# A hybrid decoder block: early column pairs of the MLP dealt out among the others, buffers and DMA order of the second MLP product rearranged

## The chip, the cores and the metric

One core of one Trainium2 chip runs the whole kernel. The metric is device time in microseconds (us) of one execution; the figure given for a kernel is the median of its timed runs. Engines are named as the profile names them: PE is the matmul engine, DVE the vector engine, ACT the scalar engine, POOL is GpSimd, and SP issues DMAs. L1120 is line 1120 of the kernel before.

## The reference, cut to what matters

```
h = RMSNorm(x); three attention branches of h, merged by gates      # first half of the kernel
x = x + merged @ w_out                                              # 1024 x 1024
h = RMSNorm(x)                                                      # gain g_mlp
hid = square(relu(h @ w_mlp_in))                                    # 1024 x 4096, "up"
x = x + hid @ w_mlp_out                                             # 4096 x 1024, "down"
return RMSNorm(x)                                                   # gain g_final
```

There are 1024 tokens of width 1024, all fp32. The change touches only what follows the branches: the output projection, the MLP and the last norm.

## The kernel before

**Products.** Every fp32 operand is split into a high part, which ACT copies with rounding (L97: `hi_…`, `th`, `sh`), and a low part, which DVE or POOL makes by a subtraction (L982: `lo_…`, `tl`, `sl`). A product is then three matmuls per step of the contraction, hi·hi, lo·hi and hi·lo (lines L152 to L154).

**The MLP by Strassen.** Both MLP products are cut in 2 x 2 blocks and made with seven block products instead of eight. In the up phase the 4096 columns of `hid` are 16 *pairs* c (128 columns from each of two neighbouring groups), and each pair needs seven products of 12 matmuls of 128x512 (`times`, output `mb_u` or `tb_u` in PSUM). The tiles `T2`, `T3`, `T4` and the halves of `h2T` are the token side. The weight side is made by `load_pair`: DMAs bring raw blocks r0 to r3, POOL adds them in four instructions (L1089 to L1092), ACT and DVE split the sums (`s23`, `s1`, `s4`, and `a1` for the unsummed block). All of r1 and r2 rotate in two buffers named `xn`, which the normalised token tiles used before; r3 and `ud` (the split s4) have one buffer each.

**Early pairs.** Two of the seven products of a pair need only token half 1. For the pairs c < EARLY they run ahead (`mb_ep`, `mb_eq`, 24 matmuls a pair) while token half 2 is being normalised, transposed (`tb_h`) and combined into T2 to T4. Their results are parked in DRAM (`p1_d`, `hid_d[0]`). In the up phase such a pair has five products (60 matmuls), any other seven (84). The up phase takes the pairs in the order 0 to 15.

**The end of a pair.** DVE adds the products, ACT does relu and square, POOL makes four differences `ta`, `tb` (L1152 to L1158), and seven blocks go to DRAM as `hid_d[k]`, k = 0 to 6, all issued by SP (L1120).

**Down phase.** The groups of blocks are [0], [5, 3], [4, 2], [6], [1]. Each block has four sub-steps sc of 48 matmuls. For a sub-step, SP loads a 1 MB raw tile `tr` from `hid_d[k][sc]` (L1218) and raw weight tiles `wr` of 0.5 MB (L1178); for the groups of two blocks POOL adds weight tiles (L1182, 40 instructions); ACT makes `sh` and `th`, DVE `sl` and `tl`, and PE multiplies (`mb_dn`, `tb_dn`). Raw `tr` tiles rotate in two buffers (`braw`), which lie in a pool that exists already in the up phase; 14 of the `wr` buffers lie in pool E, which takes the space that the up phase's pool M (T2 to T4, `stg`, `ud`) leaves.

**Last norm.** `finish` computes r = 1/rms with small DVE instructions (a Newton iteration); then one half of a token tile is scaled on DVE in one instruction, the other on ACT (x·r, L977) and POOL (·gain, L978), and both go out.

**Output projection.** It runs in four quarters (token half, column half); `load_x` brings the residual x for a quarter, 4 DMAs, at the third of four steps of the quarter.

**Order.** The code is written in program order, and a scheduler puts each engine's instructions (and SP's DMAs) into one fixed order by its own estimate of times; `band("w")` and `band("crit")` set priorities in it. On the chip every engine works its list strictly in order, so a DMA on SP waits for all those ahead of it on SP to have been issued.

Of the kernel before, what the change touches and what calls it, by code (L numbers as in the profile page):

```python
# [22 lines left out]
P = 128  # L23
# [10 lines left out]
NEG_BIG = -float(2.0 ** 117)  # L34
POS_BIG = float(2.0 ** 117)
DSA_AHEAD = 2
EARLY = 10
MERGE_WITH = (range(4), range(4, 6), range(6, 8), ())
GATE_ORDER = [*range(8), *range(16, 24), *range(8, 16)]
GATES_EARLY = 10  # L40
# [14 lines left out]
def kernel(  # L55
# [929 lines left out]
    for tg in range(2):  # L985
        ss = X3.tile([P, 2, 16], F32, tag="n_ss4", name=f"ss2_{tg}", bufs=2)[:, :, :4]
        for n in range(2):
            cs = slice(n * 512, (n + 1) * 512)
            banks = [mb_bank(f"o{tg}{n}{i}") for i in range(4)] if tg or n else first_banks
            for kp in range(KT // 2 if tg or n else 0):  # L990
                if kp == 2:
                    load_x(tg, n)
                out_part(tg, n, banks, kp)
            with band("crit"):
                for i in range(4):
                    t = 4 * tg + i
                    nc.vector.tensor_tensor(x2[:, t, cs], banks[i], x2[:, t, cs], op=ALU.add)
                    jk = X3.tile([P, 512], BF16, tag="junk", name=f"jk2_{t}{n}")
                    nc.scalar.activation(jk, x2[:, t, cs], AF.Square, accum_out=ss[:, n, i:i + 1])
        if tg:  # L1000
            ctxG.close()
            M = ctxM.enter_context(tc.tile_pool(name="M", bufs=1, side="right", reuse_waits="tile"))
            T2, T3, T4 = ([M.tile([P, 4, 512], F32R, tag=f"{nm}_{part_}", name=f"{nm}_{part_}") for part_ in ("hi", "lo")]
                          for nm in ("T2", "T3", "T4"))
        with band("crit"):
            nc.vector.tensor_tensor(ss[:, 0], ss[:, 0], ss[:, 1], op=ALU.add)
            r = rsqrt_newton(X3, ss[:, 0], 4, f"h2_{tg}")
            for i in range(4):
                t = 4 * tg + i
                ts = slice(i * P, (i + 1) * P)  # L1010
                xn = X3.tile([P, D], F32, tag="xn", name=f"xn{t}", bufs=2)
                tps = []
                for half in range(2):
                    hs = slice(half * 512, (half + 1) * 512)
                    scale_half(half, xn[:, hs], x2[:, t, hs], r[:, i:i + 1], g2[:, hs])
                    tp = tb_bank(f"h2{t}{half}")
                    for k in range(4):
                        nc.tensor.transpose(tp[:, k * P:(k + 1) * P],
                                            xn[:, (4 * half + k) * P:(4 * half + k + 1) * P], ident)
                    tpv = tp.rearrange("p (k c) -> p k c", k=4)  # L1020
# [29 lines left out]

    for c in range(EARLY):
        a11, a12 = halves(load_unit(wcol[2 * c], f"wi{2 * c}", nc.vector))
        ps1, ps2 = mb_bank(f"ep{c}"), mb_bank(f"eq{c}")
        st = M.tile([P, 2, 512], F32, tag="stg", name=f"st{c}", bufs=2)
        product(ps1, a11, B11)
        act_copy(st[:, 0], ps1)
        product(ps2, a12, B21)
        nc.vector.tensor_tensor(st[:, 1], ps2, st[:, 0], op=ALU.add)
        nc.scalar.activation(st[:, 1], st[:, 1], AF.Relu)
        nc.scalar.activation(st[:, 1], st[:, 1], AF.Square)  # L1060
        with band("w"):
            nc.sync.dma_start(p1_d[c], st[:, 0])
            nc.sync.dma_start(hid_d[0][c // 4][:, c % 4], st[:, 1])

    ring = {"n": 0}

# [32 lines left out]
    def up_pair(c):  # L1099
# [15 lines left out]
            nc.scalar.activation(v, v, AF.Relu, scale=scale)  # L1115
            nc.scalar.activation(v, v, AF.Square)

        def out_block(k, v):
            with band("w"):
                nc.sync.dma_start(hid_d[k][c // 4][:, c % 4], v)  # L1120


        last = c == NPAIR - 1
        m6 = times(s2, T2)
        if last:
            m7, m4 = times(s3, T3), times(a22, T4)
# [7 lines left out]
        if c >= EARLY:  # L1134
            vadd(c11, times(a12, B21), c11)
            square(c11)
            out_block(0, c11)
        else:
            with band("w"):
                nc.sync.dma_start(c11, hid_d[0][c // 4][:, c % 4])  # L1140
        vadd(c21, m4 if last else times(a22, T4), c22)
        m5 = times(s1, T1)
        vadd(c22, m5, c22)
        vadd(c12, m5, c12)
        square(h[:, 2:4])
        vadd(c12, times(s4, N22), c12)
        square(c12, -1.0)
        sub = partial(nc.gpsimd.tensor_tensor, op=ALU.subtract)
        ta, tb = (M.tile([P, 2, 512], F32, tag="stg", name=f"t{nm}{c}", bufs=2) for nm in ("a", "b"))
        out_block(1, c21)  # L1150
        out_block(2, c22)
        sub(ta[:, 0], c12, c11)  # L1152
        out_block(3, ta[:, 0])
        sub(ta[:, 1], c22, ta[:, 0])
# [3 lines left out]
        sub(tb[:, 1], c21, ta[:, 1])  # L1158
        out_block(6, tb[:, 1])

    for c in range(NPAIR):
        up_pair(c)

    ctxM.close()
# [6 lines left out]
    n_raw, n_op, n_bank = [0], [0], [0]  # L1171

    def w_block(i, j, c0):
        n = n_raw[0]
        n_raw[0] += 1
        pool, tag, bufs = (X3, "xn", 2) if n < 2 else ((base, "st_raw", 1), (X3, "w3_raw", 1))[n - 2] if n < 4 else (E, "wr", 14)
        raw = pool.tile([P, 2, 512], F32, tag=tag, name=f"wr{n}", bufs=bufs)
        nc.sync.dma_start(raw, w2[:, c0:c0 + 2, j - 1, (i - 1) * 512:i * 512])  # L1178
        return raw

    def add(o, a, b):
# [23 lines left out]
    def down_group(blocks, weights, evict):
# [115 lines left out]
```

## Time and profile before

| | us |
|---|---|
| timed, median of 3 runs (lowest, highest) | 1480.31 (1479.31, 1480.57) |
| the profiled execution's own time | 1476.49 |
| its span, first to last instruction | 1474.4 |
| PE busy | 1397.2 (95%) |
| DVE busy | 1041.8 (71%) |
| POOL busy | 659.4 (45%) |

The profile shows one execution, and its span is 2.1 us shorter than its own time. PE is the busiest engine by far, so the time can be read as PE's work plus the gaps in it; a gap on another engine matters only if it makes one on PE. Everything up to about 743 us runs from the same instruction lists in both kernels.

### The profile page before, as it was taken

How to read it: one execution, taken by the hardware profiler on the slowest of the kernel's cores; microseconds unless marked ns; L12 is line 12 of the kernel's file. 1: busy time of each engine (PE TensorE's matmuls, PEld its weight loads, DVE VectorE, ACT ScalarE, POOL GpSimd, SP SyncE). 2: the span in 40 equal slices, each digit the busy share in tenths (PEclk: the TensorE clock that was granted, in tenths of full speed). 3: DMA queues.
4: the chain of work that ended last, by engine and by line, in shares of the span. 5: the costliest groups of instructions: out<-in, count | busy, mean ns of one | idle time of the engine just before them, and what ended most of it. 6: DMA issues, size and time to landing. Idle time of an engine off the chain costs nothing. (4 is left out here: it accounts for less than half of the span.)

```text
span 1474.4 us, 19857 instructions
## 1 busy us (share of the span) xinstructions
PE 1397.2 (95%) x6806; PEld 1174.0 (80%) x6806; DVE 1041.8 (71%) x1871; ACT 753.4 (51%) x1397; POOL 659.4 (45%) x526
## 2 busy tenths in 40 slices
PE   6999999998899999999999999989998799999997
PEld 5788877897788898788778888777887577778885
DVE  7667999999997665756744775455444599975954
ACT  5545777875456554463535664344444333433542
POOL 4231223425667533353525236767653579730101
PEclk9999999999999999999999999999999899999999
DMA  6212331312211114346463466666445978875421
GB/s 222 86 58 83 96 103 44 97 40 62 57 44 55 58 45 145 116 147 190 159 227 102 147 191 209 203 207 207 163 151 179 363 275 276 287 256 206 170 94 57
DMA packets 169815, 216.56 MB, mean 147 GB/s; under 512 B 14036, under 2 KB 102132, under 8 KB 166132
## 3 DMA queue, kind: packets, MB, share of 16 engines
q1 hardware_dynamic: 169716, 215.31, 44.6%
q8 instruction: 53, 0.87, 0.3%
q14 instruction: 46, 0.38, 0.1%
HBM read 162.32 MB, written 52.95 MB: 146 GB/s over the span
## 5 line engine op out<-in xcount | busy, mean ns | idle before, releaser
L152 PE MATMUL gt_g<-hT_hi,hi_g 128*128 128x512 f32 x384 | 151.7, 395 | 2.8 <-DVE gs L831 2.2
L153 PE MATMUL gt_g<-hT_lo,hi_g 128*128 128x512 f32 x384 | 151.9, 396 | 0.2 <-DVE hT_lo L219 0.2
L154 PE MATMUL gt_g<-hT_hi,lo_g 128*128 128x512 f32 x384 | 151.4, 394 | 0.0
L982 DVE TENSOR_TENSOR tl<-tr,th 128x1024 fp32r<-128x1024 f32 x56 | 107.7, 1930 | 57.0 <-ACT th L97 55.1
L152 PE MATMUL mb_dn<-sh,th 128*128 128x512 f32 x336 | 132.6, 396 | 12.6 <-ACT th L97 12.6
L1182 POOL TENSOR_TENSOR wr<-wr,wr 128x1024 f32<-128x1024 f32 x40 | 123.5, 3094 | 43.7 <-DMA wr<-in_w_mlp_out_dram 42.4
L153 PE MATMUL mb_dn<-sl,th 128*128 128x512 f32 x336 | 132.9, 397 | 2.2 <-DVE sl L982 2.2
L154 PE MATMUL mb_dn<-sh,tl 128*128 128x512 f32 x336 | 130.7, 393 | 1.7 <-DVE tl L982 1.7
L97 ACT ACTIVATE th<-tr 128x1024 fp32r<-128x1024 f32 x56 | 58.5, 1051 | 137.7 <-PE tb_dn L153 114.2
L982 DVE TENSOR_TENSOR sl<-wr,sh 128x1024 fp32r<-128x1024 f32 x56 | 96.8, 1733 | 12.4 <-ACT sh L97 12.3
L544 DVE TENSOR_SCALAR_CACHE_REDUCE tk_jk<-isc,tk_c 128x384 bf16<-128x384 f32 (+3 forms) x128 | 103.5, 809 | 2.5
L111 POOL TENSOR_TENSOR lo_g<-raw_g,hi_g 128x1024 fp32r<-128x1024 f32 x24 | 58.2, 2424 | 94.6 <-ACT hi_g L97 85.7
L541 ACT ACTIVATE tk_jk<-isc,tk_c 128x1024 bf16<-128x1024 f32 x64 | 73.6, 1149 | 29.4 <-DVE tk_c L553 26.6
L97 ACT ACTIVATE hi_s<-r 128x1024 fp32r<-128x1024 f32 (+1 forms) x48 | 43.2, 911 | 85.0 <-POOL r L1090 35.6
L152 PEld LDWEIGHTS gt_g<-hT_hi,hi_g 128*128 128x128 f32 x384 | 72.4, 189 | 17.4 <-DVE gs L831 2.7
L152 PEld LDWEIGHTS mb_dn<-sh,th 128*128 128x128 f32 x336 | 64.2, 191 | 27.4 <-ACT th L97 13.9
L153 PEld LDWEIGHTS gt_g<-hT_lo,hi_g 128*128 128x128 f32 x384 | 72.4, 189 | 13.9 <-DVE hT_lo L219 0.5
L154 PEld LDWEIGHTS gt_g<-hT_hi,lo_g 128*128 128x128 f32 x384 | 72.4, 189 | 13.4
L152 PE MATMUL mb_u<-T_hi,hi_s 128*128 128x512 f32 x192 | 75.3, 392 | 7.4 <-ACT hi_s L97 7.4
L153 PEld LDWEIGHTS mb_dn<-sl,th 128*128 128x128 f32 x336 | 64.2, 191 | 17.7 <-DVE sl L982 4.6
L978 POOL TENSOR_TENSOR x<-x,g_final_t 128x512 f32<-128x512 f32 x8 | 11.4, 1431 | 148.7 <-ACT x L977 148.7
L154 PEld LDWEIGHTS mb_dn<-sh,tl 128*128 128x128 f32 x336 | 63.8, 190 | 15.9 <-DVE tl L982 2.6
(469 smaller groups left out, 4262.1 us busy)
## 6 DMA issues: line engine op xcount, KB each, us to landing
wr<-in_w_mlp_out_dram SPq DMA_DIRECT2D x80, 512.0 KB, 5.5
tr<-hid_d SPq DMA_DIRECT2D x28, 1024.0 KB, 7.1
raw_g<-in_w_in_dram SPq DMA_DIRECT2D x24, 512.0 KB, 4.0
g_d<-gs SPq DMA_DIRECT2D x48, 256.0 KB, 2.0
gl<-g_d SPq DMA_DIRECT2D x48, 256.0 KB, 3.4
hid_d<-hid SPq DMA_DIRECT2D x38, 256.0 KB, 3.5
raw_wo<-in_w_out_dram SPq DMA_DIRECT2D x16, 512.0 KB, 3.5
r<-in_w_mlp_in_dram SPq DMA_DIRECT2D x32, 256.0 KB, 3.9
```

The source lines that it names most:

```text
L97: nc.scalar.activation(o, i, AF.Copy)
L111: lo_engine.tensor_tensor(lo, raw, hi.bitcast(F32), op=ALU.subtract)
L152: nc.tensor.matmul(ps, st_hi, mv_hi, start=first, stop=False)
L153: nc.tensor.matmul(ps, st_hi, mv_lo, start=False, stop=False)
L154: nc.tensor.matmul(ps, st_lo, mv_hi, start=False, stop=last)
L541: nc.scalar.activation(jk[:, :n], isc[t], AF.Sign, bias=cand_f[:, j:j + 1], scale=-1.0, accum_out=cnt[:, j:j + 1])
L544: nc.vector.tensor_scalar(jk[:, :n], isc[t], cand_f[:, j:j + 1], 0.0, op0=ALU.is_ge, op1=ALU.add, accum_out=cnt[:, j:j + 1])
L978: nc.gpsimd.tensor_tensor(o, o, g, op=ALU.mult)
L982: engine.tensor_tensor(lo, raw, hi.bitcast(F32), op=ALU.subtract)
L1182: nc.gpsimd.tensor_tensor(o, a, b, op=ALU.add)
```

## The change

EARLY goes from 10 to 8, and the pairs are taken in the order 0, 8, 1, 9, 2, 10, ..., 7, 15, so that each five-product pair is followed by a seven-product one; `hid_d` and the rows of w_mlp_out are permuted to fit. The blocks `hid_d[0]` (of full pairs), `[1]` and `[2]` are issued by ACT's queue instead of SP's. x is loaded at the first step of a quarter, behind a DVE copy of one column per tile that depends on the quarter before. In the down phase the raw `tr` tiles rotate in five buffers (three in E, two `braw`), the `wr` tiles in other ones. In the last two groups POOL multiplies x by the gain before r is known, and the last scaling is one DVE and one ACT instruction.

```diff
-EARLY = 10
+EARLY = 8
+PAIRS = [8 * (i % 2) + i // 2 for i in range(16)]
...
     def load_x(tg, n):
         with band("w"):
+            if tg or n:
+                q = 2 * tg + n - 1
+                old = x2[:, 4 * (q // 2):4 * (q // 2) + 4, q % 2 * 512:q % 2 * 512 + 1]
+                nc.vector.tensor_copy(x2[:, 4 * tg:4 * tg + 4, n * 512:n * 512 + 1], old)
             for t in range(4 * tg, 4 * tg + 4):
...
-                if kp == 2:
+                if kp == 0:
                     load_x(tg, n)
...
-        def out_block(k, v):
-            with band("w"):
-                nc.sync.dma_start(hid_d[k][c // 4][:, c % 4], v)
+        place = PAIRS.index(c)
+        def out_block(k, v, queue=nc.sync):
+            with band("w") if queue is nc.sync else nullcontext():
+                queue.dma_start(hid_d[k][place // 4][:, place % 4], v)
...
-            out_block(0, c11)
+            out_block(0, c11, nc.scalar)
...
         square(h[:, 2:4])
+        out_block(1, c21, nc.scalar)
+        out_block(2, c22, nc.scalar)
         vadd(c12, times(s4, N22), c12)
         square(c12, -1.0)
...
-        out_block(1, c21)
-        out_block(2, c22)
...
-    for c in range(NPAIR):
+    for c in PAIRS:
         up_pair(c)
...
+    def e_tile(tag, nm, width=2, dt=F32, bufs=1):
+        return E.tile([P, width, 512], dt, tag=tag, name=nm, bufs=bufs)
...
+    first = {"t": [e_tile(f"tr{n}", f"tr_{n}", 4) for n in range(2)], "op": [op_tiles(0)]}
+    first["w"] = [e_tile("wa", "wr4", bufs=4)]
...
+    def raw_t_tile(nm):
+        n = n_tr[0]
+        n_tr[0] += 1
+        if n < 2:
+            return first["t"][n]
+        if n % 5 < 3:
+            return e_tile(f"tr{n % 5}", nm, 4)
+        return X3.tile([P, 4, 512], F32, tag="braw", name=nm, bufs=2)
+
+    def raw_w_tile():
...
+        if n < 4:
+            pool, tag, bufs = ((X3, "xn", 2), (X3, "xn", 2), (base, "st_raw", 1), (X3, "w3_raw", 1))[n]
+        elif n == 4:
+            return first["w"][0]
+        elif (n - 4) % 3 == 2:
+            pool, tag, bufs = base, ("st_hi", "st_lo")[n % 2], 2
+        else:
+            return e_tile(("wa", "wb")[(n - 4) % 12 > 5], nm, bufs=4)
...
-                    raw_t = X3.tile([P, 4, 512], F32, tag="braw", name=f"tr{k}_{sc}", bufs=2)
+                    raw_t = raw_t_tile(f"tr{k}_{sc}")
...
-            scale_half(n, o, o, r, gf[:, cs])
+            if not scaled:
+                scale_half(n, o, o, r, gf[:, cs])
+            elif n == 0:
+                nc.vector.tensor_scalar(o, o, r, 1.0, op0=ALU.mult, op1=ALU.mult)
+            else:
+                nc.scalar.activation(o, o, AF.Copy, scale=r)
...
     def e2(i, ps):
         vacc(xc(0, i, 0), ps)
         finish_half(i, 0)
-        finish(i, 0)
+        nc.gpsimd.tensor_tensor(xc(0, i, 0), xc(0, i, 0), gf[:, C1], op=ALU.mult)
+        finish(i, 0, True)
```

In the rows below, the number that ends a name is the tile's; the digits before it are those of the program's own name. **SP, at the end of the up phase, before:** `tr0_0` and `tr0_1` are the first two operands of the down phase, and `ta15`, `tb15` the last differences of the last pair.

```order
L1218 DMA tr0_0_11182<-hid_d0_0_85 128x2048
...
L1120 DMA hid_d5_3_108<-tb15_11155 128x512
L1120 DMA hid_d4_3_104<-ta15_11154 128x512
L1120 DMA hid_d6_3_112<-tb15_11155 128x512
L1218 DMA tr0_1_11252<-hid_d0_1_86 128x2048
L1178 DMA wr4_11318<-in_w_mlp_out_dram 128x2x512
...
L1178 DMA wr16_11630<-in_w_mlp_out_dram 128x2x512
L1218 DMA tr0_2_11322<-hid_d0_2_87 128x2048
L1178 DMA wr17_11634<-in_w_mlp_out_dram 128x2x512
L1218 DMA tr0_3_11392<-hid_d0_3_88 128x2048
```

**The same place after:** here the first two operands are named `tr_0` and `tr_1`.

```order
L1257 DMA tr0_3_11381<-hid_d0_3_88 128x2048
L1128 DMA hid_d3_3_100<-ta15_11145 128x512
L1128 DMA hid_d5_3_108<-tb15_11146 128x512
L1128 DMA hid_d4_3_104<-ta15_11145 128x512
L1128 DMA hid_d6_3_112<-tb15_11146 128x512
L1257 DMA tr5_0_11483<-hid_d5_0_105 128x2048
L1257 DMA tr_0_11161<-hid_d0_0_85 128x2048
L1257 DMA tr_1_11162<-hid_d0_1_86 128x2048
L1218 DMA wr4_11171<-in_w_mlp_out_dram 128x2x512
L1218 DMA wr5_11309<-in_w_mlp_out_dram 128x2x512
L1257 DMA tr0_2_11311<-hid_d0_2_87 128x2048
L1218 DMA wr7_11379<-in_w_mlp_out_dram 128x2x512
```

The first operand stood ahead of the last pair's seven outputs and now stands behind them, and behind `tr5_0`, the first operand of the second group; the third, which stood behind 13 weight tiles (wr4 to wr16), now stands behind two, and the fourth, which stood behind 14, now goes out ahead of the last differences.

**PE, from the last transposes of token half 2 (`tb_h271`) to the first up product, before:**

```order
L1018 MATMUL tb_h271_8750<-ident_127,xn7_8741 128x128 x4
L152 MATMUL mb_eq6_9011<-h2T_hi_8088,hi_wi12_9005 128x512
...
L152 MATMUL mb_eq9_9128<-h2T_hi_8088,hi_wi18_9122 128x512
L153 MATMUL mb_eq9_9128<-h2T_lo_8089,hi_wi18_9122 128x512
L154 MATMUL mb_eq9_9128<-h2T_hi_8088,lo_wi18_9123 128x512
L152 MATMUL mb_u0_1_9184<-T2_hi_8630,hi_s23_0_9171 128x512
L153 MATMUL mb_u0_1_9184<-T2_lo_8631,hi_s23_0_9171 128x512
L154 MATMUL mb_u0_1_9184<-T2_hi_8630,lo_s23_0_9172 128x512
```

**and after:**

```order
L1024 MATMUL tb_h271_8751<-ident_125,xn7_8742 128x128 x4
L153 MATMUL mb_eq6_9012<-h2T_hi_8086,hi_wi12_9006 128x512
...
L153 MATMUL mb_eq7_9051<-h2T_hi_8086,hi_wi14_9045 128x512
L154 MATMUL mb_eq7_9051<-h2T_lo_8087,hi_wi14_9045 128x512
L155 MATMUL mb_eq7_9051<-h2T_hi_8086,lo_wi14_9046 128x512
L153 MATMUL mb_u0_1_9107<-T2_hi_8631,hi_s23_0_9094 128x512
L154 MATMUL mb_u0_1_9107<-T2_lo_8632,hi_s23_0_9094 128x512
L153 MATMUL mb_u0_2_9122<-T3_hi_8633,hi_s23_0_9094 128x512
L154 MATMUL mb_u0_2_9122<-T3_lo_8634,hi_s23_0_9094 128x512
L153 MATMUL mb_u0_3_9137<-T4_hi_8635,hi_s1_0_9098 128x512
L154 MATMUL mb_u0_3_9137<-T4_lo_8636,hi_s1_0_9098 128x512
L153 MATMUL tb_u0_4_9151<-h2T_hi_8086,hi_s1_0_9098 128x512
```

Before, 81 matmuls lie between the last transposes and the first `mb_u` (9 of a product already begun and six products of 12); after, 33, since the four products of pairs 8 and 9 have moved into those pairs' turns. The first up products now begin with two matmuls each and take their third kind later.

**POOL in the up phase, around the turn from pair 2 to 3 before:**

```order
L1152 TENSOR_TENSOR ta2_9487<-hid2_9409 128x512
L1156 TENSOR_TENSOR tb2_9488<-hid2_9409 128x512
L1154 TENSOR_TENSOR ta2_9487<-hid2_9409,ta2_9487 128x512
L1089 TENSOR_TENSOR r2_4_9614<-r3_4_9615,r2_4_9614 128x512
L1091 TENSOR_TENSOR r1_4_9613<-r0_4_9612,r3_4_9615 128x512
L1158 TENSOR_TENSOR tb2_9488<-hid2_9409,ta2_9487 128x512
L1090 TENSOR_TENSOR r1_4_9613<-r2_4_9614,r0_4_9612 128x512
L1092 TENSOR_TENSOR r3_4_9615<-r0_4_9612,r1_4_9613 128x512
L1152 TENSOR_TENSOR ta3_9600<-hid3_9522 128x512
L1156 TENSOR_TENSOR tb3_9601<-hid3_9522 128x512
```

**and around the turn from pair 1 over 9 to 2 after:**

```order
L1160 TENSOR_TENSOR ta1_9445<-hid1_9365 128x512
L1164 TENSOR_TENSOR tb1_9446<-hid1_9365 128x512
L1162 TENSOR_TENSOR ta1_9445<-hid1_9365,ta1_9445 128x512
L1095 TENSOR_TENSOR r2_2_9603<-r3_2_9604,r2_2_9603 128x512
L1097 TENSOR_TENSOR r1_2_9602<-r0_2_9601,r3_2_9604 128x512
L1166 TENSOR_TENSOR tb1_9446<-hid1_9365,ta1_9445 128x512
L1096 TENSOR_TENSOR r1_2_9602<-r2_2_9603,r0_2_9601 128x512
L1098 TENSOR_TENSOR r3_2_9604<-r0_2_9601,r1_2_9602 128x512
L1160 TENSOR_TENSOR ta9_9591<-hid9_9482 128x512
L1164 TENSOR_TENSOR tb9_9592<-hid9_9482 128x512
```

The same eight instructions belong to each pair in both kernels, but now those between two five-product pairs belong to a seven-product pair.

## Rows read from the trace of the kernel before

**Rows 1.** Page, part 1: busy us, share of the span, instructions.
```profile
PE 1397.2 (95%) x6806; PEld 1174.0 (80%) x6806; DVE 1041.8 (71%) x1871; ACT 753.4 (51%) x1397; POOL 659.4 (45%) x526
```

**Rows 2.** Waits of PE, whole span: us in total, times, longest.
```profile
PE mb_dn L152 <- ACT th L97: 12.6, 3, 8.1
...
PE mb_u L152 <- ACT hi_s L97: 7.4, 5, 2.7
PE mb_o L925 <- ACT hi_wo L97: 4.2, 2, 3.0
...
PE mb_dn L153 <- DVE sl L982: 2.2, 4, 0.9
PE mb_dn L154 <- DVE tl L982: 1.7, 2, 1.2
```

**Rows 3.** Timeline of PE: start us, us, instruction, [idle before <-releaser].
```profile
855.52 0.60 PE L1018 MATMUL tb_h<-ident,xn 128*128 128x128 f32 x4
855.87 0.48 PE L152 MATMUL mb_eq<-h2T_hi,hi_wi 128*128 128x512 f32 x1
...
874.35 0.39 PE L152 MATMUL mb_u<-T_hi,hi_s 128*128 128x512 f32 x1
...
960.37 0.50 PE L152 MATMUL mb_u<-T_hi,hi_s 128*128 128x512 f32 x1 [2.75 <-ACT hi_s L97]
...
1133.62 0.39 PE L154 MATMUL mb_u<-h2T_hi,lo_s 128*128 128x512 f32 x1
1138.00 0.79 PE L152 MATMUL mb_dn<-sh,th 128*128 128x512 f32 x1 [4.00 <-ACT th L97]
```

**Rows 4.** Timelines of DVE, POOL, ACT before the up phase.
```profile
861.93 1.22 DVE L111 TENSOR_TENSOR lo_wi<-raw_wi,hi_wi 128x1024 fp32r<-128x1024 f32 x1
...
863.67 3.48 DVE L982 TENSOR_TENSOR T_lo<-xn,T_hi 128x512 fp32r<-128x512 f32 x2
...
867.37 1.29 POOL L1090 TENSOR_TENSOR r<-r,r 128x512 f32<-128x512 f32 x1 [0.78 <-DVE T_lo L982]
...
869.95 1.07 ACT L97 ACTIVATE hi_s<-r 128x1024 fp32r<-128x1024 f32 x1 [0.39 <-POOL r L1091]
```

**Rows 5.** Stretches: us, busy us by engine, granted PE clock, DMA share, GB/s.
```profile
959.50:963.20 3.70, 2.83 (x12) 2.25 (x13) 2.44 (x2) 3.70 (x6) 1.07 (x1) 1.00 0.57 158
1134.00:1138.00 4.00, 0.01 (x1) 0.00 (x0) 1.66 (x2) 3.40 (x6) 1.81 (x2) 0.81 0.35 131
1138.00:1143.30 5.30, 5.30 (x13) 4.14 (x14) 5.30 (x4) 1.84 (x2) 5.22 (x3) 0.50 0.37 138
1172.30:1177.60 5.30, 5.30 (x13) 4.25 (x14) 5.30 (x3) 2.88 (x3) 5.22 (x3) 0.52 1.02 388
```

**Rows 6.** Groups of POOL instructions, 874 to 1134 us: count, busy, mean ns.
```profile
L1091 POOL TENSOR_TENSOR r<-r,r 128x512 f32<-128x512 f32 x15 | 19.4, 1295 | 0.0
```

**Rows 7.** Timelines of POOL, SP's queue, ACT between up and down phase.
```profile
1136.19 1.27 POOL L1152 TENSOR_TENSOR ta<-hid 128x512 f32<-128x512 f32 x1 [13.95 <-ACT hid L1116]
...
1141.99 2.15 POOL L1158 TENSOR_TENSOR tb<-hid,ta 128x512 f32<-128x512 f32 x1
...
1122.75 0.32 SPq L1218 DMA_DIRECT2D tr<-hid_d  x1
...
1144.66 0.32 SPq L1218 DMA_DIRECT2D tr<-hid_d  x1
1145.03 13.22 SPq L1178 DMA_DIRECT2D wr<-in_w_mlp_out_dram  x13
1159.27 0.58 SPq L1218 DMA_DIRECT2D tr<-hid_d  x1
...
1151.14 2.01 ACT L97 ACTIVATE th<-tr 128x1024 fp32r<-128x1024 f32 x2 [2.31 <-DMA tr<-hid_d]
```

**Rows 8.** Tile tr, 1120 to 1185 us: ns min/median/max.
```profile
L982 DVE TENSOR_TENSOR tl<-tr,th x8: 1216/2305/3422, 1138.5 to 1180.8; 128x1024 fp32r<-128x1024 f32 x8
```

**Rows 9.** Timelines of ACT and POOL at the end.
```profile
1469.32 0.72 ACT L977 ACTIVATE x<-x,y_f 128x512 f32<-128x512 f32 x1 [2.48 <-DVE y_f L148]
...
1470.12 1.26 POOL L978 TENSOR_TENSOR x<-x,g_final_t 128x512 f32<-128x512 f32 x1 [1.94 <-ACT x L977]
```

More of the change, by code (lines that the diff above doesn't have):

```diff
@@ L1062 @@
             nc.sync.dma_start(p1_d[c], st[:, 0])
-            nc.sync.dma_start(hid_d[0][c // 4][:, c % 4], st[:, 1])
+            nc.sync.dma_start(hid_d[0][PAIRS.index(c) // 4][:, PAIRS.index(c) % 4], st[:, 1])
     ring = {"n": 0}
@@ L1116, in square @@
             nc.scalar.activation(v, v, AF.Square)
-        def out_block(k, v):
-            with band("w"):
-                nc.sync.dma_start(hid_d[k][c // 4][:, c % 4], v)
-        last = c == NPAIR - 1
+        place = PAIRS.index(c)
+        def out_block(k, v, queue=nc.sync):
+            with band("w") if queue is nc.sync else nullcontext():
+                queue.dma_start(hid_d[k][place // 4][:, place % 4], v)
+        last = place == NPAIR - 1
         m6 = times(s2, T2)
@@ L1136, in up_pair @@
             square(c11)
-            out_block(0, c11)
+            out_block(0, c11, nc.scalar)
         else:
             with band("w"):
-                nc.sync.dma_start(c11, hid_d[0][c // 4][:, c % 4])
+                nc.sync.dma_start(c11, hid_d[0][place // 4][:, place % 4])
         vadd(c21, m4 if last else times(a22, T4), c22)
@@ L1170, with op_tiles, w_block @@
     w2 = w_mlp_out.rearrange("(c j p) d -> p c j d", j=2, p=P)
-    n_raw, n_op, n_bank = [0], [0], [0]
-    def w_block(i, j, c0):
+    n_raw, n_tr, n_op, n_bank = [0], [0], [0], [0]
+    def e_tile(tag, nm, width=2, dt=F32, bufs=1):
+        return E.tile([P, width, 512], dt, tag=tag, name=nm, bufs=bufs)
+    def op_tiles(n):
+        return [[e_tile(f"{nm}{n % 2}", f"{nm}{n}_{q}", dt=F32R, bufs=2) for nm in ("th", "tl", "sh", "sl")] for q in range(2)]
+    first = {"t": [e_tile(f"tr{n}", f"tr_{n}", 4) for n in range(2)], "op": [op_tiles(0)]}
+    first["w"] = [e_tile("wa", "wr4", bufs=4)]
+    first["op"].append(op_tiles(1))
+    acc = e_tile("acc", "acc", 4)
+    def raw_t_tile(nm):
[7 more added lines that the diff above has]
+    def raw_w_tile():
         n = n_raw[0]
         n_raw[0] += 1
-        pool, tag, bufs = (X3, "xn", 2) if n < 2 else ((base, "st_raw", 1), (X3, "w3_raw", 1))[n - 2] if n < 4 else (E, "wr", 14)
-        raw = pool.tile([P, 2, 512], F32, tag=tag, name=f"wr{n}", bufs=bufs)
-        nc.sync.dma_start(raw, w2[:, c0:c0 + 2, j - 1, (i - 1) * 512:i * 512])
+        nm = f"wr{n}"
+        if n < 4:
[6 more added lines that the diff above has]
+            return e_tile(("wa", "wb")[(n - 4) % 12 > 5], nm, bufs=4)
+        return pool.tile([P, 2, 512], F32, tag=tag, name=nm, bufs=bufs)
+    def w_block(i, j, c0):
+        raw = raw_w_tile()
+        nc.sync.dma_start(raw, w2[:, c0 // 2::8, j - 1, (i - 1) * 512:i * 512])
         return raw
@@ L1195, in operands @@
         ops = []
-        par = n_op[0] % 2
+        n = n_op[0]
         n_op[0] += 1
-        for q, w in enumerate(ws):
-            t4 = [E.tile([P, 2, 512], F32R, tag=f"{nm}{par}", name=f"{nm}{n_op[0]}_{q}", bufs=2) for nm in ("th", "tl", "sh", "sl")]
+        for w, (q, t4) in zip(ws, enumerate(first["op"][n] if n < 2 else op_tiles(n))):
             split(t4[2], t4[3], w, nc.vector)
@@ L1227 @@
     C1, C2 = H1, H2
-    acc = E.tile([P, 4, 512], F32, tag="acc", name="acc")
     def xc(half, i, n):
@@ L1242, in finish_half, with finish @@
         nc.scalar.activation(jk, x2[:, t, (C1, C2)[n]], AF.Square, accum_out=squares[t][:, n:n + 1])
-    def finish(t, pre):
+    def finish(t, pre, scaled=False):
         ss = squares[t]
@@ L1281, in e4 @@
         finish_half(i, 1)
+        nc.gpsimd.tensor_tensor(xc(0, i, 1), xc(0, i, 1), gf[:, C2], op=ALU.mult)
     def e2(i, ps):
```

## The prediction

> **What bounds the kernel now.** I read the page first: PE is busy 1397.2 us of the 1474.4 us span [rows 1]. So some 77 us of gaps are all there is to win or lose, apart from stretches where PE is busy but its clock is low. Then the waits of PE, which give those gaps names. In the part that the change touches there are four: in the down phase 12.6 us for `th` and 3.9 us for `sl` and `tl`, in the up phase 7.4 us for `hi_s`, in the output projection 4.2 us for `hi_wo` [rows 2]. Then the timelines of PE and of those it waits for at three places: the start of the up phase, the turn from up to down, the end [rows 3, 4, 7, 9]. The pitch of a matmul of 128x512 follows from PE's timeline: 81 of them lie between 855.87 and 874.35, so 0.228 us each [rows 3]; a product of 12 is 2.73 us.
>
> One thing must be seen before the sum. A gap costs more than its length if the clock falls. After 4.0 us of idling the granted clock was 0.50 (1.2 of 2.4 GHz) for the next 5.3 us, and after the 8.1 us gap 0.52 again for 5.3 us; over the 2.75 us gap at 960 it stayed 1.00 [rows 2, 3, 5]. In 5.3 us at half clock PE does 2.65 us of work, so such a gap costs 2.65 us on top.
>
> **The change part by part.** Sums are of the profiled execution (1476.49 us), which lies 3.8 us under the median of the timed runs; I add the sum to the median, since gaps shift both alike.
>
> *x in quarters.* The loads of later quarters are issued earlier but chained; each has a quarter of the projection as cover, 96 matmuls or 21.9 us at the pitch, and three small DVE copies come in. If all the waits for `hi_wo` went, it would be -4.2 [rows 2]; but the longest, 3.0, hangs on the first quarter's x, which is not chained and is issued as before, with about as many bytes behind it. I take -0.3, between -3 and +1.
>
> *Two early pairs fewer.* PE's work is the same; its place isn't. Four products leave the stretch between the last transposes and the first up product: 33 matmuls remain, so PE stands at the up phase at 855.87 + 33 x 0.228 = 863.4 instead of 874.35 [rows 3]. What it needs there is `hi_s` of pair 0, and that was done at 869.95 + 1.07 = 871.0, covered by 3.3 us [rows 4]. Its chain is short: the POOL add L1090 waits for DVE's last `T_lo`, since r1 takes the buffer of the last token tile, then L1091, then `hi_s`. The order of the changed kernel still has the add behind that `T_lo`. What the change takes out of the chain is `lo_wi` (1.22 us on DVE, 861.93) and perhaps the slow half of the two `T_lo` (3.48 us for two [rows 4]; up to 2.1 less if they meet no POOL add). So `hi_s` is ready between 871.0 - 1.22 = 869.8 and 867.7, and PE idles 4.3 to 6.4 us. I take 5.3. As that is more than the 4.0 us after which the clock fell, I add 2.65: +8.0, between +4.3 (no fall) and +9.1.
>
> *The alternation.* In the up phase five waits for `hi_s` cost 7.4 us [rows 2], all after five-product pairs: such a pair gives PE 60 x 0.228 = 13.7 us, but POOL has eight instructions of 1.30 us for it [rows 6] in a loop with the squares and the r loads, longer than 13.7. With a seven-product pair between, the loop has 13.7 + 19.2 = 32.9 us for two such sets (20.8 us of POOL): the loop no longer limits. But three of the eight seven-product pairs (8, 10, 13) still begin with `s23`, which needs POOL's add soon after the short pair; I leave them 0.6 us each. So -7.4 + 1.7 = -5.7; at best -7.4, at worst -2.
>
> *The first two operands of the down phase.* This is the term to look at. Before, SP issued `tr0_0` at 1122.75, ahead of the last pair's outputs, so PE had it at 1138.00, 4.15 us after its last up product [rows 3, 7]. It then ran out of operands, because `tr0_2` stood behind 13 weight tiles (issued 1159.27): 8.1 us. All in all, 12.6 + 0.15 + two falls of the clock, 5.3, is 18.05 us. Now `tr_0` stands behind the last difference, which POOL can't make before the last squares: its four differences took from 1136.19 to 1144.14, and SP's next issue was at 1144.66 [rows 7]. Behind one more issue (`tr5_0`) `tr_0` goes out at 1145.05. The tr issued at 1144.66 was split from 1151.14, 6.5 us later; one more MB ahead at the 388 GB/s of [rows 5] is 2.7, so 9.2. With 1.05 us for `th` PE restarts at 1155.4: 21.5 us of idling and 2.65 of slow clock, 24.2. The later stall should be gone, for `tr0_3` is already there and `tr0_2` has two weight tiles ahead of it, and PE wants it two sub-steps (22 us) later. 24.2 - 18.05 = +6.1. Bounds: differences of 1.27 us each without DVE beside them (2.8 less) and a landing after 6.5 us give +0.6; a landing after 11.9 us, as for the tr issued at 1159.27, whose wait ended at 1172.3 [rows 5, 7] with `th` behind the landing, gives +8.8.
>
> *Raw buffers of the down phase.* Five `tr` instead of two. The waits left there, 3.9 us for `sl` and `tl` [rows 2], stand where DVE splits beside POOL's adds: a `tl` took 1.22 us at least and 3.42 at most [rows 8]. More operands ahead spread this; I take half, -2, with -3.9 as the best. At worst a sub-step of the first block, which now lies beside the adds, needs four splits of 3.42, 13.7 us, against 48 x 0.228 = 10.9 on PE: +2.8. The Trainium skill (SBUF — State Buffer, section SBUF: two separate sides) calls the ports that DVE and GpSimd share an exclusive lock for a whole instruction; the range from 1.22 to 3.42 us bears that out, and by it buffers could win nothing while both engines have a full list: this term would be 0 and the sum 2 us more, which lies within the forecast's own range.
>
> *Outputs on ACT's queue.* 40 DMAs leave SP for ACT (three for each of eight full pairs, two for each early one). SP's issue took 0.32 us [rows 7]; ACT is 51% busy [rows 1], and what waits behind them on ACT is `hi_s` of the next pair. At nothing if they fall in its idle time; if one delays every pair's `hi_s` by 0.4 us where PE waits, 16 x 0.4 = +6.4. I take 0. The Trainium skill (DMA: Bandwidth & Descriptors, section Issuing engines are not separate DMA queues) says that the issuing engine gives a transfer no engine of its own and saves only issue time; by that too the gain is about 0.
>
> *The last norm.* POOL's multiplication leaves the chain: it ended at 1471.38, ACT's x·r at 1470.04, so at most -1.3 [rows 9]; POOL's multiplications now beside the small DVE instructions may take some back. -1.1.
>
> Sum: -0.3 + 8.0 - 5.7 + 6.1 - 2 + 0 - 1.1 = +5.0; 1480.3 + 5.0 = **1485.3 us**.
>
> **The rivals.** (1) *The start is milder.* The POOL chain ends earlier than I think and PE idles about 3 us, at which the clock held: the start costs 3 instead of 8, the sum is 0, 1480.3. For it: nothing on DVE but splits stands in the chain. Against: the order of POOL and DVE. 0.2. (2) *Faster: pair 0's weights are ready when PE comes.* It decides at `hi_s` done by 863.7, 7.3 us earlier than before. Then the start costs nothing: 5.0 - 8.0 = -3.0, 1477.3; each us that the differences or the landing at the turn fall short of my values comes off that. For it: the chain's POOL adds wait for a DVE split, which is short when nothing stands beside it. Against: the last transposes are at the same place in PE's list, so 2.1 us of shortened splits and 1.22 would have to become 7. With the case that the turn is at its lower bound (+0.6, sum -0.5) and the down phase at its best (-2.4), I give the fast side 0.2. (3) *ACT's queue hurts.* ACT stalls on its DMAs while PE waits for `hi_s`: up to 1485.3 + 6.4 = 1491.7. 0.15. My forecast: 0.45, with 1481.5 to 1489 as its own range.
>
> **How the numbers follow.** A measurement of this kernel can tell about 0.2%, 3 us. Slower: most of the forecast (0.42) and rival 3, 0.57. Same: rival 1 and the lower end of the forecast, 0.23. Faster: 0.2. The range reaches from a little under rival 2, 1475.5, to rival 3, 1491.
>
> **What would show it.** Right: a PE wait for `hi_s` of over 4 us near 863 with a granted clock of about 0.5 behind it; no waits over 1 us for `hi_s` after seven-product pairs; one gap of about 21 us ahead of the first `mb_dn` and none of 8 us after it; ACT's or DVE's last scaling, not a POOL multiplication, as the end of the computation. Wrong: a first `mb_dn` within 12 us of the last `mb_u`, or a start of the up phase without a gap, and the kernel is faster; waits for `hi_s` at every pair, and it is slower than I say.

## The result, and the profile after

The changed kernel takes 1491.93 us (median of 4 runs, 1489.18 to 1493.01) against 1480.44 for the kernel before in the same measurement: a ratio of 1.0076, 95% interval 1.0059 to 1.0094. It is 11.5 us slower; 5.0 were forecast. The execution profiled took 1489.18 us, its span is 1487.5 against 1474.4.

The waits of PE, over the whole span, answer to [rows 2]:

```profile
PE mb_dn L153 <- ACT th L98: 20.1, 1, 20.1
PE mb_u L153 <- ACT hi_s L98: 12.1, 3, 5.8
...
PE mb_o L926 <- ACT hi_wo L98: 3.9, 2, 2.9
```

The waits for `sl` and `tl` are gone. The three of the down phase for `th` have become one of 20.1 us, and `hi_s` now costs 12.1 instead of 7.4 us, in three waits. PE's timeline shows where they stand, and answers to [rows 3]:

```profile
871.16 0.79 PE L153 MATMUL mb_u<-T_hi,hi_s 128*128 128x512 f32 x1 [5.83 <-ACT hi_s L98]
...
1006.71 0.50 PE L153 MATMUL mb_u<-T_hi,hi_s 128*128 128x512 f32 x1 [2.50 <-ACT hi_s L98]
...
1111.71 0.80 PE L153 MATMUL mb_u<-T_hi,hi_s 128*128 128x512 f32 x1 [3.81 <-ACT hi_s L98]
...
1146.91 0.39 PE L155 MATMUL mb_u<-h2T_hi,lo_s 128*128 128x512 f32 x1
1167.40 0.79 PE L153 MATMUL mb_dn<-sh,th 128*128 128x512 f32 x1 [20.10 <-ACT th L98]
```

The granted clock behind each of these gaps, from the table of stretches (columns as in [rows 5]; the last stretch is one without a gap, for comparison):

```profile
752.40:757.80 5.40, 5.33 (x17) 4.29 (x18) 2.45 (x2) 1.08 (x2) 0.00 (x0) 0.71 0.93 322
871.10:876.40 5.30, 5.24 (x15) 4.22 (x16) 2.96 (x3) 1.48 (x3) 0.14 (x1) 0.63 0.67 193
1006.70:1012.00 5.30, 5.14 (x14) 3.81 (x15) 3.86 (x5) 2.96 (x4) 0.22 (x1) 0.68 0.79 240
1111.70:1117.00 5.30, 5.29 (x13) 4.13 (x14) 3.86 (x5) 2.97 (x4) 0.21 (x1) 0.50 0.86 254
...
1240.00:1265.00 25.00, 25.00 (x112) 20.71 (x111) 14.36 (x8) 7.82 (x8) 13.36 (x5) 1.00 0.57 197
```

PE stays "busy" in the first four rows, but at 0.50 to 0.71 of the clock it does 13 to 17 matmuls in 5.3 us instead of 23. So the gap of 2.5 us cost 4.5: nine matmuls of 0.227 us on top of itself.

Cut into stretches by four marks on PE's timeline (last `tb_h`, first and last up product's matmul, first and last matmul of the down phase), the two executions compare so:

| stretch | before | after | change, less 10.9 us of moved work | forecast |
|---|---|---|---|---|
| to the last transposes | 855.5 | 857.2 | +1.7 | -0.3 |
| to the first up matmul | 18.8 | 13.9 | +6.0 | +5.3 |
| to the last up matmul | 259.3 | 275.8 | +5.6 | -5.7, and +2.65 for the clock |
| to the first down matmul | 4.4 | 20.5 | +16.1 | +17.4 |
| to the last down matmul | 325.0 | 306.9 | -18.0 | -13.3 |
| to the end of the span | 11.4 | 13.1 | +1.7 | -1.1 |

(48 matmuls of 0.227 us left the second stretch and came into the third. 17.4 is 21.5 less 4.15; -13.3 is 8.6 us of waits, 2.65 of slow clock and 2.) The changes add up to 13.1, the difference of the spans. The largest miss is the up phase. There the forecast left no wait over 1 us after the start, and there are two, of 2.5 and 3.8 us, with a fall of the clock each, both behind a seven-product pair (11 and 14).

The first of them can be followed back through the timelines of ACT, SP's queue and POOL (and the second, 105 us later, reads alike: POOL idles 10.05 us for r3 ahead of 1082.89, and the next pair's `tb` starts at 1102.09):

```profile
975.15 0.63 ACT L1122 ACTIVATE hid<-hid 128x512 f32<-128x512 f32 x1 [0.50 <-ACT hid L1121]
...
973.93 0.37 SPq L1092 DMA_DIRECT2D r<-in_w_mlp_in_dram  x1
...
967.46 1.30 POOL L1098 TENSOR_TENSOR r<-r,r 128x512 f32<-128x512 f32 x1
978.80 2.20 POOL L1095 TENSOR_TENSOR r<-r,r 128x512 f32<-128x512 f32 x1 [10.05 <-DMA r<-in_w_mlp_in_dram]
...
982.21 1.29 POOL L1160 TENSOR_TENSOR ta<-hid 128x512 f32<-128x512 f32 x1
...
989.46 2.28 POOL L1166 TENSOR_TENSOR tb<-hid,ta 128x512 f32<-128x512 f32 x1
993.44 1.30 POOL L1160 TENSOR_TENSOR ta<-hid 128x512 f32<-128x512 f32 x1 [1.69 <-ACT hid L1122]
997.07 1.29 POOL L1164 TENSOR_TENSOR tb<-hid 128x512 f32<-128x512 f32 x1 [2.33 <-DVE hid L1143]
...
999.56 1.29 POOL L1095 TENSOR_TENSOR r<-r,r 128x512 f32<-128x512 f32 x1
...
1004.31 1.26 POOL L1096 TENSOR_TENSOR r<-r,r 128x512 f32<-128x512 f32 x1
...
989.53 0.38 SPq L1094 DMA_DIRECT2D r<-in_w_mlp_in_dram  x1
990.01 0.54 SPq L1093 DMA_DIRECT2D r<-in_w_mlp_in_dram  x1
991.77 0.34 SPq L1128 DMA_DIRECT2D hid_d<-tb  x1
...
1005.60 1.06 ACT L98 ACTIVATE hi_s<-r 128x1024 fp32r<-128x1024 f32 x1 [2.48 <-POOL r L1096]
...
DMA to landing us min/median/max: 5.2/5.2/5.2
```

POOL has nothing to do from 968.8 to 978.8, because the next instruction in its list, the first weight add for pair 11, waits for r3, which SP could issue only at 973.93. But the squares of pair 10 were done at 975.8, and its four differences stand behind two of these adds: the first starts at 982.21, the last ends at 991.7. SP sends that last one off at 991.77, and its DMA lands 5.2 us later (the last row). `ta` and `tb` of all pairs share two buffers (`stg`), so the next pair's `tb` starts at 997.07 only, and behind it in POOL's list stand the adds for pair 4: 999.56, 1004.31, then ACT's `hi_s` at 1005.60, then PE at 1006.71. (The profile puts POOL's wait until 997.07 down to an add of DVE that ended just before; that add, L1143, writes the `hid` of pair 11, and this `tb` reads that of pair 3. The DMA landed at 991.77 + 5.2, about 997.0.) ACT is not what held `hi_s`: it had been idle for 2.48 us and waited for POOL.

The turn to the down phase answers to [rows 7], POOL, SP and ACT in that order:

```profile
1155.56 2.13 POOL L1166 TENSOR_TENSOR tb<-hid,ta 128x512 f32<-128x512 f32 x1
...
1157.71 0.32 SPq L1128 DMA_DIRECT2D hid_d<-tb  x1
1158.21 1.29 SPq L1257 DMA_DIRECT2D tr<-hid_d  x3
...
1166.29 2.00 ACT L98 ACTIVATE th<-tr 128x1024 fp32r<-128x1024 f32 x2 [12.83 <-DMA tr<-hid_d]
```

The first `tr` goes out behind the last difference, as the order said, and `th` follows 8.1 us after the first of three issues.

The end answers to [rows 9]; POOL's multiplications by the gain, and three instructions of DVE:

```profile
1474.49 1.26 POOL L1329 TENSOR_TENSOR x<-x,g_final_t 128x512 f32<-128x512 f32 x1 [2.03 <-ACT jk L1279]
1478.29 1.26 POOL L1329 TENSOR_TENSOR x<-x,g_final_t 128x512 f32<-128x512 f32 x1 [2.55 <-ACT jk L1279]
...
1474.52 1.24 DVE L149 SCALAR_TENSOR_TENSOR y_f<-t_f,y_f 128x1 f32<-128x1 f32 x1
...
1476.72 0.68 DVE L1271 TENSOR_TENSOR x<-x,tb_dn 128x512 f32<-128x512 f32 x1
...
1478.33 1.25 DVE L145 SCALAR_TENSOR_TENSOR t_f<-y_f,hv_f 128x1 f32<-128x1 f32 x1
```

The 1.24 and 1.25 us are instructions of DVE on 128 x 1 elements, which take 0.16 and 0.22 otherwise. Each starts with a multiplication of POOL and ends with it. The last add of x starts at 1476.72, 2.4 us after PE's last matmul started, instead of 0.6.

### The profile page after: what moved, and what is told of

The parts are those of the page before. It is cut to its first block, busy times and chain, and to the rows that moved or that the text cites. A ratio compares the mean times of both kernels' runs of the same rounds, so it can differ in the third digit from the quotient of the medians.

```text
span 1487.5 us, 19865 instructions
## 1 busy us (share of the span) xinstructions
PE 1402.3 (94%) x6806; PEld 1182.1 (79%) x6806; DVE 1042.7 (70%) x1874; ACT 754.8 (51%) x1397; POOL 670.4 (45%) x530
## 4 chain that ended last, share of the span: by engine, by line
PE 65%; DVE 17%; issue 5%; POOL 4%; ACT 4%; DMA 4%; SPq 0%; ACTq 0%; POOLq 0%; DVEq 0%
PE mb_dn L153 5%; PE mb_dn L154 5%; PE mb_dn L155 5%; PE mb_o L926 4%; PE mb_u L153 4%; PE mb_u L154 4%; PE gt_g L154 4%; PE mb_u L155 4%; PE gt_g L155 4%; PE gt_g L153 4%; DVE tk_jk L545 3%; PE tb_dn L154 2%; PE tb_dn L153 2%; PE tb_dn L155 2%; PE gt_p L153 1%
## 5 line engine op out<-in xcount | busy, mean ns | idle before, releaser
L1222 POOL TENSOR_TENSOR wr<-wr,wr 128x1024 f32<-128x1024 f32 x40 | 118.9, 2984 | 86.2 <-DMA wr<-in_w_mlp_out_dram 77.2
L153 PE MATMUL mb_dn<-sh,th 128*128 128x512 f32 x336 | 131.8, 392 | 20.1 <-ACT th L98 20.1
L988 DVE TENSOR_TENSOR tl<-tr,th 128x1024 fp32r<-128x1024 f32 x56 | 98.9, 1768 | 65.8 <-ACT th L98 63.7
L988 DVE TENSOR_TENSOR sl<-wr,sh 128x1024 fp32r<-128x1024 f32 x56 | 104.0, 1862 | 6.2 <-ACT sh L98 6.2
L988 DVE TENSOR_TENSOR lo_s<-r,hi_s 128x1024 fp32r<-128x1024 f32 (+1 forms) x48 | 61.1, 1291 | 50.0 <-ACT hi_s L98 49.9
L153 PEld LDWEIGHTS mb_dn<-sh,th 128*128 128x128 f32 x336 | 63.6, 189 | 33.8 <-ACT th L98 20.5
L153 PE MATMUL mb_u<-T_hi,hi_s 128*128 128x512 f32 x192 | 78.1, 407 | 12.1 <-ACT hi_s L98 12.1
L154 PE MATMUL mb_u<-T_lo,hi_s 128*128 128x512 f32 x192 | 77.1, 401 | 0.0
L155 PE MATMUL mb_u<-T_hi,lo_s 128*128 128x512 f32 x192 | 74.5, 398 | 0.1
```

What stands on the lines that cost most here:

```text
L153: nc.tensor.matmul(ps, st_hi, mv_hi, start=first, stop=False)
L154: nc.tensor.matmul(ps, st_hi, mv_lo, start=False, stop=False)
L155: nc.tensor.matmul(ps, st_lo, mv_hi, start=False, stop=last)
L988: engine.tensor_tensor(lo, raw, hi.bitcast(F32), op=ALU.subtract)
L1222: nc.gpsimd.tensor_tensor(o, a, b, op=ALU.add)
```

## The experiments

**Theory Q:** the up phase loses time because the outputs' move to ACT's queue changed the order of POOL's list: weight adds of pairs 11 and 14 ahead of the differences of pairs 10 and 13. **Rivals:** the alternation itself (A), or what ACT's queue does on the chip (its issues hold ACT, or its transfers come at another time).

**1. Outputs on SP again, all else as changed.**

```diff
-            out_block(0, c11, nc.scalar)
+            out_block(0, c11)
...
-        out_block(1, c21, nc.scalar)
-        out_block(2, c22, nc.scalar)
+        out_block(1, c21)
+        out_block(2, c22)
```

> The changed kernel with the outputs of blocks 0, 1 and 2 issued by SP again. Theory Q: the two late waits for hi_s in the up phase (2.5 us at 1006.7, 3.8 us at 1111.7, each with a fall of the clock behind it) come from POOL's list, in which the weight adds of pairs 11 and 14 stand ahead of the differences of pairs 10 and 13 and wait 10 us for a DMA; that order came with the move to ACT's queue. Then both waits are under 1 us here, the up phase (276.0 us from first to last product) is 265 to 268, and the kernel is 7 to 12 us faster than the changed one: 1480 to 1485. Rival A: the alternation itself makes them (the short pair behind a long one always finds POOL behind): the waits stay, the time is within 3 us of the changed kernel's 1491.9. Rival D: SP can't carry the outputs as well, r comes later and new waits appear: over 1492.

1479.43 us, ratio to the kernel before 0.9989 (0.9974 to 1.0004): 12.5 less than the changed kernel, a little more than expected. The up phase is 263.6 us against 275.8. Waits of PE from the last transposes on:

```profile
PE mb_dn L153 <- ACT th L98: 20.5, 1, 20.5
PE mb_u L153 <- ACT hi_s L98: 5.9, 1, 5.9
```

Only the wait at the start is left for `hi_s`. A is out: the alternation is the same here. So is D: no new wait appears. It is not yet said whether the order or the queue did it.

**2. Outputs still on ACT's queue, POOL's order repaired.** Two lines are written a little later; nothing returns to SP.

```diff
         square(h[:, 2:4])
-        out_block(1, c21, nc.scalar)
-        out_block(2, c22, nc.scalar)
         vadd(c12, times(s4, N22), c12)
         square(c12, -1.0)
+        out_block(1, c21, nc.scalar)
+        out_block(2, c22, nc.scalar)
```

POOL's list at pair 10, changed kernel and this one:

```
changed:  r2_11  r1_11  ta10  tb10  r1_11  ta10  r3_11  tb10
here:     ta10   tb10   r2_11 r1_11 ta10   r1_11 tb10   r3_11
```

> The changed kernel with all outputs of blocks 0, 1 and 2 still on ACT's queue, but blocks 1 and 2 written behind the square of c12 instead of ahead of it. In the order that comes out, POOL's first differences of pairs 10 and 13 stand ahead of the adds of pairs 11 and 14 again, as with the outputs on SP. If POOL's order is the cause: no wait for hi_s over 1 us after the start, the up phase (275.8 us from first to last product) is 263 to 266, the time 1478 to 1484. If the issuing on ACT itself is the cause (ACT held by its DMAs, or the transfers' place among the others): waits of 2 us and more for hi_s stay in the up phase and the time is 1488 or more.

1480.76 us, 1.0003 (0.9988 to 1.0017). The waits near 1007 and 1112 are gone. One wait of 2.6 us is there that was not expected, with its fall of the clock, so the up phase is 268.4 and not 263 to 266. POOL at pair 10, and PE's one wait with the `hi_s` of ACT that ended it:

```profile
976.91 1.29 POOL L1160 TENSOR_TENSOR ta<-hid 128x512 f32<-128x512 f32 x1 [6.64 <-ACT hid L1122]
978.16 1.29 POOL L1164 TENSOR_TENSOR tb<-hid 128x512 f32<-128x512 f32 x1
980.14 1.30 POOL L1095 TENSOR_TENSOR r<-r,r 128x512 f32<-128x512 f32 x1 [0.69 <-POOL tb L1164]
...
986.15 2.28 POOL L1166 TENSOR_TENSOR tb<-hid,ta 128x512 f32<-128x512 f32 x1
...
1053.62 1.06 ACT L98 ACTIVATE hi_s<-r 128x1024 fp32r<-128x1024 f32 x1 [3.33 <-POOL r L1096]
...
1054.73 0.50 PE L153 MATMUL mb_u<-T_hi,hi_s 128*128 128x512 f32 x1 [2.64 <-ACT hi_s L98]
```

Pair 10's first difference now starts 1.2 us after its squares and the last ends at 988.4. With every output still on ACT, the time is within 1.5 us of the first run's: the order of POOL's list cost the 11 to 12.5 us, not the issuing on ACT. (The edit also moves a few entries of DVE's, ACT's and SP's lists. That POOL's are the ones that count rests on the chain read above.) The remaining wait is at the first products of pair 13, one of the three full pairs that begin with `s23`, for which the forecast had left 0.6 us each. It is not ACT's issuing either: ACT had been idle for 3.33 us and waited for POOL, whose add L1096 took 2.25 us there beside a split of DVE, against 1.33 in run 1, and whose first add for that pair had waited 0.65 us for a DMA. What makes POOL late there was not tested.

**3. The alternation alone, on the kernel before.** EARLY 8, the new order of pairs, and the places in `hid_d` and w_mlp_out that go with it.

> The kernel before with EARLY 8 and the alternating order alone. Theory Q: the start of the up phase costs 5 to 6.5 us of idling and 2 to 2.7 of slow clock, the alternation gives back 4 to 7 of the 9.2 us that the up phase loses: 0 to +4 us, 1480 to 1485, with no wait for hi_s over 1 us after the start. Rival A: the up phase still has waits of 2 us and more in it and the total is +8 or more, 1488 to 1493.

1479.86 us, 0.9991 (0.9976 to 1.0006). The waits from the last transposes on:

```profile
PE mb_dn L153 <- ACT th L98: 13.6, 2, 9.6
PE mb_u L153 <- ACT hi_s L98: 5.6, 2, 5.4
```

5.4 of the 5.6 us are the start. The up phase takes 264.3 us, 253.4 without the moved work, against 259.3 to 262.0 in the five kernels of this study with the old up phase. So the alternation gives back 6 to 8.6 us, the slow clock at its start already taken off, and the gap at the start takes 5.5: no gain and no loss, at the lower end of the expectation.

**4. The new buffers of the down phase alone, on the kernel before.** The lines of `e_tile` to `raw_w_tile` and `operands`.

> The kernel before with the new buffers of the down phase alone. By the two traces: the gap at the turn grows from 4.2 to about 20 us (+16), all waits after it go (-18): -4 to +1 us, 1476 to 1481. Rival: the down phase owes its smooth run to the order of the weights or the late start and not to the buffers; then waits for sl, tl and th stay and the time is +8 us or more.

1482.43 us, 1.0015 (1.0000 to 1.0031), a little above the expectation. The first down matmul comes 21.1 us after the last up one (4.4 before), the down phase takes 310.8 instead of 325.0. So the gap eats what the buffers give. One wait of 2.1 us for `sl` with a slow clock behind it (0.68 over 5.3 us, so 1.7 us) remains, which the changed kernel has not; the two make 3.8 us, and its down phase is 3.9 us longer than the changed kernel's.

**5. The same with the first two raw tiles in `braw`.**

```diff
-        if n < 2:
-            return first["t"][n]
-        if n % 5 < 3:
-            return e_tile(f"tr{n % 5}", nm, 4)
+        if n in (2, 3):
+            return first["t"][n - 2]
+        if n % 5 > 1:
+            return e_tile(f"tr{n % 5 - 2}", nm, 4)
```

> As the run with the new buffers alone, but the first two raw tiles lie in braw, so that the first operand goes out ahead of the last pair's outputs again; the three in E take numbers 2 to 4. If the gap at the turn hangs on the place of the first operand in SP's list alone: it is about 4 us again, the wait of 8.1 us and its fall of the clock stay away, and the kernel is 10 to 17 us faster than before: 1463 to 1470. Rival: the second operand, now behind the last difference, is late, PE waits over 5 us for it at the second sub-step and the clock falls again: 1472 to 1480.

1467.73 us, 0.9908 (0.9889 to 0.9926): 13 us faster than before. The last up and the first down matmul, and the waits of PE in the down phase:

```profile
1139.60 0.39 PE L154 MATMUL mb_u<-h2T_hi,lo_s 128*128 128x512 f32 x1
1143.98 0.50 PE L152 MATMUL mb_dn<-sh,th 128*128 128x512 f32 x1 [4.00 <-ACT th L97]
...
PE mb_dn L152 <- ACT th L97: 5.0, 2, 4.0
PE mb_dn L153 <- DVE sl L982: 1.4, 1, 1.4
```

The gap is 4.0 us again, and the down phase still takes 310.5: the gain of the buffers and the loss at the turn come apart, and the place of one DMA, that of the first operand, decides over 16 us of gap.

**6. The new last norm alone, on the kernel before.**

> The kernel before with the new last norm alone. Theory P: POOL's multiplications hold small DVE instructions beside them for about 1.25 us each (three in the last 8 us), so the last add of x comes 1 us later and the stretch from the last matmul's start to the end of the span grows from 11.4 to 12.6 to 13.3 us: the kernel is 1 to 2 us slower, 1480 to 1483. Rival, the prediction's step: the stretch shrinks by 1.1 to 10.3, 1479.

The stretch from the last matmul to the end is 13.2 us, as in the changed kernel (13.1), against 11.4. The time, 1483.38 us or 1.0011 (0.9998 to 1.0024), agrees but does not tell 1.8 us from nothing.

**7. The gain on POOL for the first finished half only.** In the last group no POOL instruction is left; DVE scales its half by r and gain in one instruction.

```diff
-            scale_half(n, o, o, r, gf[:, cs])
+            if scaled and n:
+                nc.scalar.activation(o, o, AF.Copy, scale=r)
+            else:
+                scale_half(n, o, o, r, gf[:, cs])
...
-        finish(i, 0)
+        finish(i, 0, True)
```

(`e4` multiplies its half by the gain on POOL as in the change.)

> The kernel before, with the gain multiplied ahead on POOL only for the half that the last but one group finishes; the other half is scaled by DVE in one instruction as before, and the last group has no POOL instruction. Theory P: nothing holds DVE at the end, the stretch from the last matmul's start to the end is 9.8 to 10.4 instead of 11.4, the time 1 to 1.6 us less, 1478 to 1480. If POOL is not what holds DVE, the stretch is as long as with the new norm, 12 us or more.

1479.61 us, 0.9991 (0.9978 to 1.0003). The end takes 10.2 us after the last matmul instead of 11.4 (13.2 with both halves, run 6): PE's last matmul, DVE's last add, DVE's last scaling:

```profile
1466.44 0.39 PE L154 MATMUL tb_dn<-sh,tl 128*128 128x512 f32 x1
...
1467.06 0.68 DVE L1234 TENSOR_TENSOR x<-x,tb_dn 128x512 f32<-128x512 f32 x1
...
1472.13 0.75 DVE L975 SCALAR_TENSOR_TENSOR x<-x,y_f,g_final_t 128x512 f32<-128x512 f32 x1
```

The add follows the start of the last matmul after 0.6 us again. P holds by this stretch; the total can't show 1 us.

**8. A combination.** EARLY 10 again, but the six full pairs dealt out among the ten early ones; outputs on SP; buffers as in run 5; norm as in run 7; x loaded at the third step of a quarter and without the DVE copy, as in the kernel before.

```diff
+PAIRS = [0, 10, 1, 2, 3, 11, 4, 5, 6, 12, 7, 13, 8, 14, 9, 15]
```

> EARLY 10 with the six full pairs dealt out among the ten early ones (0, 10, 1, 2, 3, 11, 4, 5, 6, 12, 7, 13, 8, 14, 9, 15), outputs on SP, the new buffers with the first two raw tiles in braw, and the last norm of the run with one half. Theory: the start of the up phase is covered (no gap, no fall of the clock), the up phase loses under 4 us instead of 9, the turn stays at 4.4 us, the down phase at about 310, the end at 10.2: 1457 to 1463. Rival: three early pairs in a row are enough for the waits to come back, and the up phase loses as much as before: 1466.

1460.49 us (1455.26 to 1462.33), 0.9852 (0.9825 to 0.9879): 20.8 us faster than the kernel before and 31 faster than the changed one, as expected. The rival, an up phase as slow as before, is out. The first up matmul comes 18.8 us after the last transposes, as before and without a gap; the up phase takes 254.1 us against 259.3 or more; turn, down phase and end take 4.4, 309.0 and 10.4. PE's waits:

```profile
PE mb_dn L153 <- ACT th L98: 4.0, 1, 4.0
PE mb_u L153 <- ACT hi_s L98: 2.8, 2, 2.2
```

## Why the prediction was wrong

**The step that failed** is "Outputs on ACT's queue. [...] At nothing if they fall in its idle time; [...] I take 0." It priced what ACT would do with 40 DMAs, and run 2, with all of them still on ACT, shows that price to be near nothing, as I took it. But it did not ask what else the edit moves. The scheduler answered it with another order of POOL's list, and that order was there to be read: the excerpt of POOL's list ahead of the prediction shows pairs 1 and 9, where it is harmless, and not pair 10. By run 1 the edit cost 12.5 us, and in the two traces the up phase is 12.2 us longer with it. Without it the kernel takes 1479.4 us, 5.9 under the forecast, so "slower" came out by a cause that the forecast did not name. Rival 3 ends at 1491.7, 0.2 us from the measured time; that is luck. It had the right place (waits for `hi_s` in the up phase) and the wrong mechanism: ACT was idle and waited for POOL.

**The alternation** (-5.7) was right in mechanism and too small: -6 to -8.6 in run 3 even with the slow clock at its start.

**The start** (+5.3, and 2.65 for the clock) was right in size: PE idled 5.83 us in the changed kernel and 5.87, 4.55 and 5.35 in runs 1 to 3, with a clock of 0.50 to 0.63 over the 5.3 us behind it, which is 2.0 to 2.65 us. The chain was read rightly only in part. POOL in the changed kernel:

```profile
866.31 1.27 POOL L988 TENSOR_TENSOR T_lo<-braw,T_hi 128x512 fp32r<-128x512 f32 x1 [3.36 <-ACT T_hi L98]
867.54 1.26 POOL L1096 TENSOR_TENSOR r<-r,r 128x512 f32<-128x512 f32 x1
```

DVE's last two `T_lo` took 1.28 us instead of 3.48 and had ended at 866.45, so they no longer set the add. L1096 follows POOL's own last `T_lo`, which waited for ACT's `T_hi`; the forecast has no such step.

**The turn** (+17.4 for the gap) was right to about 1 us: +16.1. **The buffers** (-2) were mis-sized. 8.6 us of later waits for `th`, their fall of the clock and all 3.9 us for `sl` and `tl` went. The down phase is 18.0 us shorter in the changed kernel, where even the best of the range gives 8.6 + 2.65 + 3.9 = 15.15; with the buffers alone it is 14.1 shorter, within that. The expected limit, DVE's splits beside POOL's adds, is no limit where operands are ready well ahead: 35 of DVE's 112 splits `tl` and `sl` took over 2 us in the changed kernel, 34 before, and PE no longer waits for them. So "buffers could win nothing" is not borne out here.

**The last norm** (-1.1) has the wrong sign: +1.7. I had named the cause ("beside the small DVE instructions may take some back") and given it too little: the multiplication leaves the chain, but POOL's other multiplications hold DVE, twice at the very end by about 1 us. Of the 1.7 us, 1.0 is there when SP issues the last output (9.5 us after the last matmul's start instead of 8.5); the other 0.7 comes behind that issue, and no run explains it. The Trainium skill (SBUF — State Buffer, section SBUF: two separate sides) says of the ports shared by DVE and GpSimd that the loser waits for the whole instruction of the other. The rows agree: 1.24 and 1.25 us on DVE beside 1.26 on POOL, ending together.

**The x quarters** (-0.3) can't be told from these runs. The gap at 752 us was 3.05 us before and 2.92 after; most of the +1.7 us, 1.5, is the clock, which fell after the one (0.71 over 5.3 us) and not after the other. It fell in run 3 too, which has the old loads, and there the last transposes came at 857.2 as well.

What stays open: why run 4 has its wait of 2.1 us for `sl` and the changed kernel has none, and where some 2.6 of the 18.0 us in the changed kernel's down phase come from, which the named waits (8.6 and 3.9) and the clock (2.9: two falls of 0.50 and 0.52 before, one of 0.57 after) leave over.

## What to carry to other kernels

Where a scheduler writes the lists, read every engine's list over the whole stretch that an edit lies in, above all for an instruction that waits for a late DMA and now stands ahead of work that is ready: an edit that relieves one queue can be paid for on another engine. Ask of a new buffer not only how many there are but whose memory it was, since one DMA that moves behind the end of a phase can cost as much as all the prefetching behind it wins. Work that leaves a chain for an engine that holds up the chain's own engine is still on it.

## What the runs showed of the hardware that I had not expected

The granted clock after a short gap is not settled by the gap's length. It fell after the gaps of 2.50 and 2.92 us of the changed kernel (0.68 and 0.71 in the 5.3 us behind them) and not after those of 2.75 and 3.05 us of the kernel before. Over the ten traces, from 735 us on, it fell after 11 of the 20 gaps of 2.1 to 3.1 us. With 1.4 to 2.0 us for each of these falls (14 to 17 matmuls in 5.3 us instead of 23), a few such gaps could make much of the spread of a kernel's times (1476.3 to 1483.5 us in the ten executions of run 3); that was not tested.
